# Fewer cached-key steps beside the attention, scans ahead of sums on VectorE, and norm rows in PSUM for the last output layer

## The chip, the core and the metric

The kernel runs on one core of one Trainium2 chip. The metric is device time of one launch in microseconds; a lower one is better. TensorE (PE) multiplies matrices into PSUM, VectorE (DVE) and ScalarE (ACT) read and write PSUM and SBUF, GpSimd (POOL) works in SBUF alone, and SyncE (SP) issues nearly all DMAs from one queue in order.

## The reference

One inference step of a two-layer trunk of width 1024, for a prompt of 1024 positions and for 8 samples with one new position each. Both groups share the weights. Layer 0 projects to q, k, v, a gate, a pooling input u and its gate. The attention is stick-breaking, with 8 heads of 64:

```
z = q.k / 8 + bias
w[t,s] = sigmoid(z[t,s]) * prod over s<j<t of (1 - sigmoid(z[t,j]))
o_a = w @ v ;  o_b = pooled(u) @ w_pool * scale
x1  = layer_norm(ALPHA*x + concat(o_a*silu(g_a), o_b*silu(g_b)) @ w_out)
```

For a sample, the keys and values are 4096 cached rows in 32 pages found through a page table. Layer 1 is a gated depthwise convolution of 31 taps with a layer norm and SiLU, a gate, an output projection and again `layer_norm(ALPHA*x + ...)`. Outputs are both groups' rows, the new k and v, and the pooling and convolution states.

## The kernel before

Matrix products in float32 are made of three products of split operands (`whi*xh + wlo*xh + whi*xl`, L225 to L227 and L1029 to L1031). ACT makes the high part, POOL (or DVE) the low part `wlo` (L210) or `xl` (L196).

Instructions of PE, ACT, DVE and POOL stand in the order in which the program writes them; each engine takes them in that order. So a waiting instruction holds up all that is behind it on its engine.

**The attention stage** (L947 to L981) goes through 48 units of up to 512 keys, 12 for each of four pairs of heads. For a unit, `z_a` has PE form scores and ACT form two sigmoids for each of two heads. `z_b` has DVE run the product scan (L365) and the product with the sigmoid (L369, L371) into `sg`. One unit later `tpart` transposes `sg` on PE (L845), and two units later `ppart` multiplies with v (L861). Between these slots, `fill.part` runs pieces of the projection of later heads.

**The decode of cached keys** is a generator, `decode_k`. `tick(n)` advances it by n steps. A full step issues the DMA of two pages of keys (`kt`, 512 KB, four buffers), multiplies the pages that were issued two steps earlier by the query row (L417), and sums products of the step before that over each head on DVE (L409). There are 64 full steps for each of two halves of the samples. The multiplication is on POOL in 7 of 8 steps and on DVE in the eighth (`KMOD`, `KPOOL`). A half ends with about ten short steps: transposes, sigmoids, one scan over 1024 elements (L437), carries between rows (L443 to L447), and one product over 1023 (L454).

In the stage a unit gets `TBASE + TSLOPE*(384-n)/384` steps for n keys. Over the 48 units this comes to 134 steps; 8 are made before the stage, and each half has 77, and one step stands ahead of them. The steps that are left then go one by one between the 32 groups of layer 0's output projection (`out_layer`, `between`), and the rest behind them.

**`out_layer`** does 32 groups, each of 24 matmuls for 128 rows by 256 columns. DVE adds the residual (L1062) and collects statistics (L1066). After a block's fourth group the norm follows: `norm_s` on DVE and POOL (`rs`, L1001, L1002), `norm_a` on DVE, `norm_b` on ACT and POOL (L1020, L1021), or on DVE (L1018) for the blocks in `FAST`. In layer 0 the gain row is in PSUM (`gps`); in layer 1 it is in SBUF. Weight quarters are converted by `conv_w` at groups 0 to 3 and 12 to 19.

**Between convolution and layer 1's output** the means and variances are spread over partitions by PE (`mid_a`), applied by DVE (`mid_b`), then SiLU, gate and split follow. `mid_a` takes its PSUM tile from `trp()`, which has two buffers there and four after `swap_psum("pzd", 4)`. The convolution's accumulator has its own two banks under the tag `conv`.

Of the kernel before, what the change touches and what calls it, by code (L numbers as in the profile page):

```python
# [14 lines left out]
F32 = mybir.dt.float32  # L15
# [3 lines left out]
AF = mybir.ActivationFunctionType  # L19
ALU = mybir.AluOpType  # L20
AX = mybir.AxisListType
SP = mybir.EngineType.SP
PSUM = bass.MemoryType.PSUM

P = 128
D = 1024
S = 1024
# [18 lines left out]
KS = 30  # L46
PS_ = 15
NEG = -1e30
KMOD = 8
KPOOL = 7  # L50
ENG = mybir.EngineType
KLAG = 2
DTB = 2
# [12 lines left out]
WRB = 3  # L66
ETICK = 0.35
EDVE = (1, 2, 3, 0)
TBASE = 2.8
TSLOPE = 1.5  # L70
NHEADS = (0, 6, 6, 6, 6, 6, 6, 6)
SNY = 7
# [12 lines left out]
SNZ = 5  # L85
HALVES = (3, 6)
OLAG = 3
FAST = (5, 6, 7)
WCONVA = ((0, 5), (1, 5))
SY = 2  # L90
VRATE = 1.575
# [9 lines left out]
def kernel(  # L101
# [9 lines left out]
    pe, act, dve, gp, sp = nc.tensor, nc.scalar, nc.vector, nc.gpsimd, nc.sync  # L111
# [8 lines left out]
    w_out1 = w_out_c[0]  # L120
# [11 lines left out]
    pz = [pap.enter_context(tc.tile_pool(name="pza", bufs=1, space=PSUM))]  # L132
    NZT = [5]

    def psum(tag, bufs, shape=(P, 512), dt=F32):
        return (psq[0] if tag == "qv" else ps).tile(list(shape), dt, tag=tag, name=tag, bufs=bufs)
# [3 lines left out]
    def acc():  # L140
        deep[1] += 1
        if deep[0] and deep[1] % deep[0] == 0:
            return trp()
        return psum("acc", 2)

    def trp():
        return pz[0].tile([P, 512], F32, tag="zt", name="zt", bufs=NZT[0])

    def swap_psum(name, n):
        pzp.close()  # L150
        pz[0] = pzp.enter_context(tc.tile_pool(name=name, bufs=1, space=PSUM, reuse_waits="tile"))
        NZT[0] = n
# [236 lines left out]
    def decode_k():  # L389
        qrow = {0: query_rows(0)}  # L390
        yield
        for hf in range(2):
# [5 lines left out]
            for s in range(len(units) + KLAG + 1):  # L398
# [13 lines left out]
                if KLAG <= s < len(units) + KLAG:  # L412
                    bi, j = units[s - KLAG]
                    b = hf * 4 + bi
                    kt = kts[s - KLAG]
                    eng = gp if (j // 2) % KMOD < KPOOL else dve
                    eng.tensor_tensor(out=kt, in0=kt, in1=qrow[b], op=ALU.mult)  # L417
# [53 lines left out]
    def tick(n):  # L471
        while n > 0 and queue:
            try:
                next(queue[0])
                n -= 1
            except StopIteration:
                queue.pop(0)
# [353 lines left out]
    def z_b(u):  # L831
        pair, qb, c0, c1, first, last = units[u]
        for hh in range(2):
            z, kp = st["z", u][hh]
            st["w", u, hh], st["prev", hh] = stick_b(z, kp, c1 - c0, None if first else st["prev", hh])
# [56 lines left out]
    t = trp()  # L892
# [23 lines left out]
    for i, q in enumerate(qorder):  # L916
# [3 lines left out]
        o = acc()[:, 0:n]  # L920
# [26 lines left out]
    for u in range(len(units) + 2):  # L947
        if u < len(units):
            pair, qb, c0, c1, first, last = units[u]
            n = c1 - c0  # L950
            if u % 12 == 0:
                fill.until(f"v{pair}")
                fleft = 42 if pair < 3 else 45
                fbase = fleft / 12.0
            fcred += fbase
            tcred += TBASE + TSLOPE * (384 - n) / 384.0
            z_a(u)
        k = int(tcred)
        tcred -= k
        f = min(int(fcred), fleft)  # L960
        fcred -= f
        fleft -= f
        fs = [(f + 2 - i) // 3 for i in range(3)]

        def slot(i):
            if i == PAT and u > 1:
                ppart(u - 2)
            if i == TAT and 0 < u <= len(units):
                tpart(u - 1)

        slot(0)
        fill.part(fs[0])
        tick((k + 1) // 2)
        if u < len(units):
            z_b(u)
        slot(1)
        fill.part(fs[1])
        slot(2)
        tick(k // 2)
        fill.part(fs[2])  # L980
        slot(3)  # L981
# [23 lines left out]
    def norm_a(gb, y, mv, halves, gps):  # L1005
        if gps:
            for i in range(2):
                h = slice(i * 512, i * 512 + 512)
                dve.scalar_tensor_tensor(out=y[:, h], in0=y[:, h], scalar=mv[:, 0:1], in1=gps[i],
                                         op0=ALU.subtract, op1=ALU.mult)  # L1010
            return
        for h in halves:
            dve.scalar_tensor_tensor(out=y[:, h], in0=y[:, h], scalar=mv[:, 0:1], in1=gb[:, 0, h],
                                     op0=ALU.subtract, op1=ALU.mult)

    def norm_b(gb, y, rs, fast, h):
        if fast:
            dve.scalar_tensor_tensor(out=y[:, h], in0=y[:, h], scalar=rs, in1=gb[:, 1, h], op0=ALU.mult, op1=ALU.add)  # L1018
        else:
            act.activation(out=y[:, h], in_=y[:, h], func=AF.Copy, scale=rs)  # L1020
            gp.tensor_tensor(out=y[:, h], in0=y[:, h], in1=gb[:, 1, h], op=ALU.add)  # L1021
# [10 lines left out]

    def out_layer(w, first, ahead, X, gb, pool, finish, between, before=None, half=None, tail=None, lag=OLAG, fast0=FAST, wide=0, gps=()):
        order = [(n4, tb) for t0 in (0, 4) for n4 in range(2) for tb in range(t0, t0 + 4)]
        for i in range(NTB + lag):
            if i < NTB:
                order.append((2, i))
            if i >= lag:
                order.append((3, i - lag))
        dmas = {0: (1, 3)} | {9 + i: (2, i) for i in range(4)} | {13 + i: (3, i) for i in range(4)}  # L1040
        convs = {i: (1, i) for i in range(4)} | {12 + i: (2, i) for i in range(4)} | {16 + i: (3, i) for i in range(4)}
        raws, sts = {}, {}
        tiles = {0: first, 1: [], 2: [], 3: []}

        def fetch(q, i):
            raws[q, i] = dma_quarter(w, q, i)

        for i in range(3):
            raws[1, i] = ahead[i]
        for s, (n4, tb) in enumerate(order):  # L1050
            f0 = n4 * 256
            if s in convs:
                q, i = convs[s]
                tiles[q].append(conv_w(raws[q, i], 2, 256, pool if q % 2 else None, dve if q == 1 and i % 2 and fast0 is FASTB else None))
            if s in dmas:
                fetch(*dmas[s])
            if before is not None:
                before(n4, tb)
            o = (trp() if s < wide and s % 3 else acc())[:, 0:256]
            out_group(tiles[n4], o, tb, half)  # L1060
            y = X[tb]
            dve.scalar_tensor_tensor(out=y[:, f0:f0 + 256], in0=y[:, f0:f0 + 256], scalar=ALPHA,  # L1062
                                     in1=o, op0=ALU.mult, op1=ALU.add)
            if n4 == 0:
                sts[tb] = pool.tile([P, 4, 6], F32, tag="st", name="st", bufs=NTB)
            dve.bn_stats(sts[tb][:, n4, :], y[:, f0:f0 + 256])  # L1066
            if n4 == 3:
                fast = tb in fast0
                halves = (slice(0, 512), slice(512, 1024)) if tb >= 6 else (slice(0, 1024),)
                mv, rs = norm_s(pool, sts[tb])  # L1070

                def app(y=y, mv=mv, rs=rs, tb=tb, fast=fast, halves=halves):
                    norm_a(gb[0], y, mv, halves, gps)
                    for h in halves:
                        norm_b(gb[0], y, rs, fast, h)
                        finish(tb, y, h)
                defer((DTC if fast0 is FASTB else DTD)[tb], app)
            between(n4, tb)
            point()
            if tail is not None:  # L1080
                tail(n4, tb)
# [4 lines left out]
    X = {}  # L1086
# [80 lines left out]
    rows = [(w_out0, 0, k) for k in range(NK)]  # L1167
# [347 lines left out]
    BC = {}  # L1515
# [34 lines left out]

    def mid_a(c):
        a, b = MID[c]
        t = trp()
        for i, tb in enumerate(range(a, b)):
            pe.transpose(out=t[:, i * P:(i + 1) * P], in_=rmf[:, tb:tb + 1].broadcast_to([P, P]), identity=ident)
            pe.transpose(out=t[:, 256 + i * P:256 + (i + 1) * P], in_=rvf[:, tb:tb + 1].broadcast_to([P, P]),
                         identity=ident)
        BC[c] = t
# [31 lines left out]
    X = {}  # L1590
# [5 lines left out]
            X[tb] = C[:, tb].rearrange("p k c -> p (k c)")  # L1596
            sp.dma_start(X[tb], x1_dram[tb * P:(tb + 1) * P, :])

    gb1 = [None]

    def before(n4, tb):
        if (n4, tb) in STEPS:
            STEPS[n4, tb]()
        if n4:
            return
        if tb == 3:
            gb1[0] = G[:, 0:2].rearrange("p t k c -> p t (k c)")
            sp.dma_start(gb1[0][:, 0, :], ln_c_g.to_broadcast([P, D]))
            sp.dma_start(gb1[0][:, 1, :], ln_c_b.to_broadcast([P, D]))
# [22 lines left out]
    mid_c(0)  # L1632
    mid_g(1)
    flush()
    swap_psum("pzd", 4)
    cxp.close()
    dx = ctx.enter_context(tc.tile_pool(name="dx", bufs=1, reuse_waits="tile"))
    fill.part(2)
# [9 lines left out]
    first1 = load_first(w_out1, range(2)) + late1  # L1648
    ahead1 = [dma_quarter(w_out1, 1, i) for i in range(3)]
# [3 lines left out]
    mid_g(2)  # L1653
    flush()
    deep[0] = DEEPD
    out_layer(w_out1, first1, ahead1, X, gb1, dx, fin1, lambda n4, tb: tick(1), before, lambda: tick(1))
    while queue:
        tick(1)
    flush()
# [24 lines left out]
```

## Time and profile before

| | us |
|---|---|
| median of 3 runs | 1143.98 |
| lowest and highest | 1140.2 and 1145.24 |
| the profiled execution | 1143.3 |
| its span, first to last instruction | 1141.5 |

| engine | busy us | share of span |
|---|---|---|
| PE | 1051.7 | 92% |
| DVE | 812.6 | 71% |
| POOL | 665.1 | 58% |
| ACT | 491.9 | 43% |

Times count from the span's start. The attention stage runs from about 68 to 497, layer 0's output projection from about 515 to 625, the convolution layer from there to about 1000, and layer 1's output projection to the end. Busy time is an average over these stages, so each is read by itself. PE's mean granted clock over the span is 0.971 of its upper level.

### The profile page before, as it was taken

To read this page: it belongs to the slowest core of one execution; us is meant where nothing else is said; L and a number is where in the kernel's file an instruction comes from. 1 tells how busy PE (TensorE), PEld (TensorE's weight loads), DVE (VectorE), ACT (ScalarE), POOL (GpSimd) and SP (SyncE) were. 2 spreads that over 40 slices of the span, in tenths; PEclk is the share of its full clock that TensorE was granted. 3 is DMA by queue.
4 is the path that set the end of the run, shared out by engine and by line. 5 is a ranking of instruction groups with operands and counts; after the bars stand their busy time and mean duration, and the time that the engine had idled before them with its cause. 6 is when DMAs were issued, how large, how long until landed. Compare 5 with 4: busy or idle time off the path is not lost.

```text
span 1141.5 us, 19830 instructions
## 1 busy us (share of the span) xinstructions
PE 1051.7 (92%) x6804; PEld 841.7 (74%) x6804; DVE 812.6 (71%) x961; ACT 491.9 (43%) x929; POOL 665.1 (58%) x502
## 2 busy tenths in 40 slices
PE   8998888889999998797998999999999999899994
PEld 7897777768877877697997666566666466677784
DVE  3458878688599898767348399999999960484246
ACT  4345465547565565571204224444544422462210
POOL 3277879691788889872418336765766612343235
PEclk9999999999999999898999999999999999899997
DMA  8577767783467976655203887787687678386922
GB/s 267 170 230 231 243 194 222 207 251 98 141 217 219 278 216 216 199 194 203 68 26 142 240 253 249 234 252 217 194 266 236 210 237 264 122 280 218 322 102 113
DMA packets 179206, 235.20 MB, mean 206 GB/s; under 512 B 15418, under 2 KB 95939, under 8 KB 179081
## 3 DMA queue, kind: packets, MB, share of 16 engines
q1 hardware_dynamic: 179105, 233.94, 65.1%
q8 instruction: 53, 0.87, 0.3%
q14 instruction: 48, 0.39, 0.1%
HBM read 212.60 MB, written 16.14 MB: 200 GB/s over the span
## 4 chain that ended last, share of the span: by engine, by line
PE 54%; POOL 13%; DVE 11%; issue 9%; DMA 7%; ACT 3%; SPq 3%; POOLq 0%; DVEq 0%; ACTq 0%
PE acc L225 11%; PE acc L227 10%; PE acc L226 10%; POOL kt L417 7%; PE qv L1151 5%; DMA kt<-in_cache_k_dram 3%; DVE zw L409 3%; PE acc L1029 3%; POOL wlo L210 2%; PE acc L1031 2%; PE acc L1030 2%; DVE kp L365 2%; DMA vt<-in_cache_v_dram 1%; DVE xl L196 1%; POOL xres L1021 1%
## 5 line engine op out<-in xcount | busy, mean ns | idle before, releaser
L225 PE MATMUL acc<-xh,whi 128*128 128x384 f32 (+2 forms) x960 | 361.5, 377 | 11.5 <-DVE hbt L705 5.7
L227 PE MATMUL acc<-xl,whi 128*128 128x384 f32 (+2 forms) x960 | 340.4, 355 | 0.2 <-DVE xl L196 0.2
L226 PE MATMUL acc<-xh,wlo 128*128 128x384 f32 (+2 forms) x960 | 339.7, 354 | 0.0
L417 POOL TENSOR_TENSOR kt<-kt,qbs 128x1024 f32<-128x1024 f32 x112 | 274.1, 2464 | 39.6 <-DMA kt<-in_cache_k_dram 30.0
L210 POOL TENSOR_TENSOR wlo<-wraw,whi 128x512 fp32r<-128x512 f32 x122 | 161.6, 1328 | 184.1 <-ACT whi L205 179.5
L1373 DVE SCALAR_TENSOR_TENSOR conv_acc<-hbuf,wdwT,conv_acc 128x1024 f32<-128x1024 f32 x196 | 252.8, 1290 | 6.8
L225 PEld LDWEIGHTS acc<-xh,whi 128*128 128x128 f32 x960 | 184.3, 192 | 78.1 <-issue 26.1
L409 DVE TENSOR_REDUCE zw<-kt 128x16 f32<-128x1024 f32 x128 | 153.6, 1212 | 63.5 <-POOL kt L417 63.3
L227 PEld LDWEIGHTS acc<-xl,whi 128*128 128x128 f32 x960 | 184.3, 192 | 18.0 <-DVE xl L196 0.7
L226 PEld LDWEIGHTS acc<-xh,wlo 128*128 128x128 f32 x960 | 185.0, 193 | 15.7 <-issue 0.3
L1363 POOL TENSOR_TENSOR conv<-conv,tap 128x512 f32<-128x512 f32 x84 | 105.9, 1293 | 17.6 <-ACT tap L1360 17.6
L1029 PE MATMUL acc<-whi,xh 128*128 128x256 f32 x352 | 102.4, 291 | 0.0
L1031 PE MATMUL acc<-whi,xl 128*128 128x256 f32 x352 | 99.5, 283 | 2.1 <-DVE xl L196 2.1
L1030 PE MATMUL acc<-wlo,xh 128*128 128x256 f32 x352 | 99.4, 282 | 0.0
L365 DVE TENSOR_TENSOR_SCAN kp<-kp,zt 128x512 f32<-128x512 f32 (+3 forms) x96 | 92.4, 963 | 1.2 <-ACT zt L361 1.2
L205 ACT ACTIVATE whi<-wraw 128x512 fp32r<-128x512 f32 x126 | 77.4, 624 | 32.1 <-DMA wraw<-in_w_out_ab_dram 14.1
L360 ACT ACTIVATE kp<-zt,nbiash 128x512 f32<-128x512 f32 (+3 forms) x96 | 55.8, 581 | 71.4 <-DVE sg L371 40.7
L1360 ACT ACTIVATE tap<-hbuf,wdwT 128x512 f32<-128x512 f32 x84 | 59.7, 721 | 48.0 <-POOL conv L1363 38.1
L1151 PE MATMUL qv<-vt,zw 128*32 128x512 f32 x512 | 76.1, 604 | 3.1 <-DMA vt<-in_cache_v_dram 3.1
L1029 PEld LDWEIGHTS acc<-whi,xh 128*128 128x128 f32 x352 | 66.8, 190 | 7.9 <-issue 7.4
L1031 PEld LDWEIGHTS acc<-whi,xl 128*128 128x128 f32 x352 | 67.0, 190 | 2.3 <-DVE xl L196 2.3
L845 PE MATMUL zt<-ident,sg 128*128 128x128 f32 x288 | 44.7, 286 | 24.2 <-DVE sg L371 12.9
(274 smaller groups left out, 1507.3 us busy)
## 6 DMA issues: line engine op xcount, KB each, us to landing
kt<-in_cache_k_dram SPq DMA_DIRECT2D x256, 256.0 KB
vt<-in_cache_v_dram SPq DMA_DIRECT2D x256, 256.0 KB
wraw<-in_w_in_c_dram SPq DMA_DIRECT2D x48, 256.0 KB
vt<-in_w_in_c_dram SPq DMA_DIRECT2D x48, 256.0 KB
wraw<-in_w_in_ab_dram SPq DMA_DIRECT2D x46, 256.0 KB
xt<-in_x_prompt_dram SPq DMA_DIRECT2D x8, 512.0 KB
wraw<-in_w_out_ab_dram SPq DMA_DIRECT2D x16, 256.0 KB
xres<-in_x_prompt_dram SPq DMA_DIRECT2D x8, 512.0 KB
```

The costliest lines, as they stand in the source:

```text
L210: (eng or gp).tensor_tensor(out=lo, in0=raw, in1=hi.bitcast(F32), op=ALU.subtract)
L225: pe.matmul(o, hi[:, k % 4, :], xh, start=(k == 0), stop=False)
L226: pe.matmul(o, lo[:, k % 4, :], xh, start=False, stop=False)
L227: pe.matmul(o, hi[:, k % 4, :], xl, start=False, stop=(k == NK - 1))
L365: dve.tensor_tensor_scan(out=kr, data0=kr, data1=z[:, 0:1].broadcast_to([P, n]), initial=1.0 if prev is None else prev, op0=ALU.mult, op1= ...
L409: dve.tensor_reduce(out=seg[:, j // 8, j % 8:j % 8 + 2, bi * 8:bi * 8 + 8], in_=kts.pop(s - KLAG - 1).rearrange("p a (h d) -> p a h d", d=DH),
L417: eng.tensor_tensor(out=kt, in0=kt, in1=qrow[b], op=ALU.mult)
L1029: pe.matmul(o, XH[:, k, cs], hi[:, k % 2, :], start=(k == 0), stop=False)
L1030: pe.matmul(o, XH[:, k, cs], lo[:, k % 2, :], start=False, stop=False)
L1031: pe.matmul(o, XL[:, k, cs], hi[:, k % 2, :], start=False, stop=(k == NK - 1))
L1151: pe.matmul(pv[32 * bi:32 * bi + 32, :], Z[:, j % 8 * 4 + j // 8, :], vts[bi], start=(j == 0), stop=(j == NPG - 1), tile_position=(0, 32 * ...
L1373: dve.scalar_tensor_tensor(out=part[1], in0=hb[:, j:j + S], scalar=w, in1=part[1], op0=ALU.mult, op1=ALU.add)
```

## The change

It changes four things. In the decode, every fourth multiplication goes to DVE (before, every eighth), and a unit gets a base of 2.35 steps (before 2.8): 112 steps in the stage for 134. Within a unit, `z_b` stands ahead of the first `tick`. In layer 1's output projection the gain row is copied to two PSUM banks and `norm_a` reads it there; blocks 5 and 7 use the new `norm_fast`, which keeps the value between its two passes in PSUM, and block 6 leaves the blocks whose second pass is on DVE. For these banks `trp()` has three buffers for four there, and `mid_a` of the first two parts writes to the convolution's two banks.

```diff
-KMOD = 8
-KPOOL = 7
+KMOD = 4
+KPOOL = 3
-TBASE = 2.8
+TBASE = 2.35
-FAST = (5, 6, 7)
+FAST = (5, 7)
...
         fill.part(fs[0])
-        tick((k + 1) // 2)
         if u < len(units):
             z_b(u)
+        tick((k + 1) // 2)
         slot(1)
...
+    def norm_fast(gb, y, mv, rs, h, i, gps):
+        t = trp()
+        dve.scalar_tensor_tensor(out=t, in0=y[:, h], scalar=mv[:, 0:1], in1=gps[i], op0=ALU.subtract, op1=ALU.mult)
+        return lambda: dve.scalar_tensor_tensor(out=y[:, h], in0=t, scalar=rs, in1=gb[:, 1, h], op0=ALU.mult, op1=ALU.add)
...
                 def app(y=y, mv=mv, rs=rs, tb=tb, fast=fast, halves=halves):
+                    if fast and gps:
+                        hs = (slice(0, 512), slice(512, 1024))
+                        bs = [norm_fast(gb[0], y, mv, rs, h, i, gps) for i, h in enumerate(hs)]
+                        for h, b in zip(hs, bs):
+                            b()
+                            finish(tb, y, h)
+                        return
                     norm_a(gb[0], y, mv, halves, gps)
...
     def mid_a(c):
         a, b = MID[c]
-        t = trp()
+        if c == 0:
+            BC["wide"] = pz[0].tile([P, S], F32, tag="conv", name="rows", bufs=1)
+        t = BC["wide"][:, c * 512:c * 512 + 512] if c < 2 else trp()
...
+        if (n4, tb) == (2, 4):
+            gps1.extend((psum("o", 1), pg.tile([P, 512], F32, name="scale1")))
+            for i in range(2):
+                act.activation(out=gps1[i], in_=gb1[0][:, 0, i * 512:i * 512 + 512], func=AF.Copy)
...
-    swap_psum("pzd", 4)
+    swap_psum("pzd", 3)
+    pg = ctx.enter_context(tc.tile_pool(name="pg", bufs=1, space=PSUM, reuse_waits="tile"))
...
-    out_layer(w_out1, first1, ahead1, X, gb1, dx, fin1, lambda n4, tb: tick(1), before, lambda: tick(1))
+    out_layer(w_out1, first1, ahead1, X, gb1, dx, fin1, lambda n4, tb: tick(1), before, lambda: tick(1), gps=gps1)
```

## Rows read from the trace of the kernel before

**Rows 1.** Three stretches: busy PE, PEld, DVE, ACT, POOL; PE clock; DMA share, GB/s.

```profile
68.00:497.00 429.00, 382.92 (x2621) 332.13 (x2620) 343.00 (x416) 240.93 (x504) 334.61 (x183) 0.96 0.69 213
531.00:590.00 59.00, 59.00 (x493) 58.83 (x493) 19.80 (x43) 9.57 (x18) 12.80 (x13) 0.99 0.21 67
590.00:640.00 50.00, 45.80 (x312) 39.81 (x310) 32.23 (x57) 20.39 (x32) 32.62 (x43) 1.00 0.46 153
```

**Rows 2.** Waits of PE, 68 to 497: us in total, times, longest.

```profile
PE zt L845 <- DVE sg L371: 12.9, 7, 3.2
PE zt L845 <- DVE sg L369: 10.8, 10, 2.4
PE acc L225 <- DVE hbt L705: 5.7, 4, 2.3
PE acc L225 <- DVE kl L611: 5.5, 2, 3.4
PE zt L815 <- DVE sg L371: 4.9, 1, 4.9
```

**Rows 3.** Waits of DVE, 68 to 497.

```profile
DVE zw L409 <- POOL kt L417: 60.2, 32, 5.4
...
DVE kp L365 <- ACT zt L361: 1.2, 1, 1.2
```

**Rows 4.** Timeline of DVE in one unit: start, us, instruction, idle before.

```profile
193.45 1.22 DVE L409 TENSOR_REDUCE zw<-kt 128x16 f32<-128x1024 f32 x1 [3.34 <-POOL kt L417]
```

**Rows 5.** Groups by line, 75 to 525: count, busy, mean ns, idle before.

```profile
L417 POOL TENSOR_TENSOR kt<-kt,qbs 128x1024 f32<-128x1024 f32 x106 | 259.9, 2469 | 39.3 <-DMA kt<-in_cache_k_dram 29.7 <-DVE kp L365 3.9 <-DVE zw L409 3.2
...
L409 DVE TENSOR_REDUCE zw<-kt 128x16 f32<-128x1024 f32 x123 | 147.7, 1212 | 57.4 <-POOL kt L417 57.1
...
L417 DVE TENSOR_TENSOR kt<-kt,qbs 128x1024 f32<-128x1024 f32 x16 | 28.1, 1756 | 0.0
```

**Rows 6.** The decode's multiplication, line 417: count, ns min/median/max.

```profile
L417 POOL TENSOR_TENSOR kt<-kt,qbs x112: 2337/2392/3387, 54.2 to 515.4; 128x1024 f32<-128x1024 f32 x112
L417 DVE TENSOR_TENSOR kt<-kt,qbs x16: 1209/1276/3224, 79.5 to 524.8; 128x1024 f32<-128x1024 f32 x16
```

**Rows 7.** Timeline of PE: first score product, four units apart.

```profile
274.50 0.63 PE L815 MATMUL zt<-km,qh 128*128 128x512 f32 x2
...
305.91 0.62 PE L815 MATMUL zt<-km,qh 128*128 128x512 f32 x2
```

**Rows 8.** Timeline of DVE in layer 0's output groups.

```profile
538.34 2.27 DVE L437 TENSOR_TENSOR_SCAN kpd<-kpd 128x1024 f32<-128x1024 f32 x1
...
546.15 0.42 DVE L1062 SCALAR_TENSOR_TENSOR xres<-xres,acc 128x256 f32<-128x256 f32 x1 [2.06 <-PE acc L1031]
546.61 0.43 DVE L1066 BATCH_NORM_STATS2 st<-xres 128x6 f32<-128x256 f32 x1
...
552.62 1.27 DVE L454 SCALAR_TENSOR_TENSOR zw<-kpd,car,zw 128x1023 f32<-128x1023 f32 x1
```

**Rows 9.** Timeline of POOL, layer 0's output groups.

```profile
559.98 1.29 POOL L210 TENSOR_TENSOR wlo<-wraw,whi 128x512 fp32r<-128x512 f32 x1 [3.70 <-ACT whi L205]
```

**Rows 10.** Timeline of SP's queue, start of layer 0's output groups.

```profile
508.08 11.08 SPq L1092 DMA_DIRECT2D xres<-in_x_prompt_dram  x2
```

**Rows 11.** Timeline of DVE: a norm's first pass from PSUM, then the end.

```profile
590.78 0.73 DVE L1009 SCALAR_TENSOR_TENSOR xres<-xres,mv,o 128x512 f32<-128x512 f32 x1
...
1118.98 1.27 DVE L1013 SCALAR_TENSOR_TENSOR conv<-conv,mv,gate 128x1024 f32<-128x1024 f32 x1
...
1122.67 3.58 DVE L1013 SCALAR_TENSOR_TENSOR conv<-conv,mv,gate 128x1024 f32<-128x1024 f32 x2
...
1137.09 1.41 DVE L1018 SCALAR_TENSOR_TENSOR conv<-conv,rs,gate 128x512 f32<-128x512 f32 x2 [0.45 <-POOL rs L1002]
```

**Rows 12.** Timeline of PE between convolution and layer 1's output.

```profile
987.79 0.45 PE L1555 MATMUL zt<-ident,rmu 128*128 128x128 f32 x1 [5.68 <-DVE conv L1567]
...
1012.30 0.38 PE L1031 MATMUL acc<-whi,xl 128*128 128x256 f32 x1 [2.09 <-DVE xl L196]
```

More of the change, by code (lines that the diff above doesn't have):

```diff
@@ L1597, in mid_c @@
             sp.dma_start(X[tb], x1_dram[tb * P:(tb + 1) * P, :])
-    gb1 = [None]
+    gb1, gps1 = [None], []
     def before(n4, tb):
```

## The prediction

> **What bounds the kernel now.** I read the stretches first. The attention stage lasts 429 us, and TensorE is busy for 383 of it [rows 1]; the other 46 us are what a change of order can win there. DVE is busy for 343 us and POOL for 335. Next come TensorE's waits in that stretch: 12.9 + 10.8 + 4.9 = 28.6 us for `sg`, the outcome of a unit's scans, and 5.7 + 5.5 = 11.2 us for two smaller results of DVE [rows 2]. So 39.8 of the 46 us are waits for DVE. Then DVE's own waits: it sits for 60.2 us in front of the decode's sum, waiting for POOL's multiplication, and for 1.2 us before a scan whose sigmoid is late [rows 3]. Busy and held together DVE is taken for about 403 of 429 us. The timeline shows how one becomes the other: at 193.45 a sum starts after 3.34 us of waiting for POOL, and the scans stand behind it in program order [rows 4]. The stage is bound by a chain of POOL, DVE and TensorE, each full at other moments, and not by TensorE's work.
>
> What it could reach: between the halves of the decode, where few sums are made, four units take 305.91 - 274.50 = 31.4 us, or 7.85 us each [rows 7], against 429 / 48 = 8.94 on average. Over 48 units that is 52 us less.
>
> Behind the stage, layer 0's output groups are bound by TensorE: 59.00 of 59 us, with POOL busy for 12.8 and the DMA moving 67 GB/s [rows 1].
>
> All sums stand against the profiled execution: 1143.3 us, its span of 1141.5 and 1.8 around it. The median of the runs is 0.7 above it, so no correction is made.
>
> **The change part by part.**
>
> *Decode in the stage.* 134 - 112 = 22 steps leave it. Each takes a sum of 1.212 us off DVE [rows 5]: 26.7 us. Of the multiplications, 106 were on POOL and 16 on DVE [rows 5], 122 in all; 100 stay, 75 on POOL and 25 on DVE. POOL goes from 259.9 to 75 x 2.469 = 185 us, which is 75 less. DVE gets 9 more of them at 1.756 us, the mean of the sixteen [rows 5] (the median is 1.276, the longest 3.224 [rows 6]): 15.8 us. DVE's net is 26.7 - 15.8 = 11 us less. POOL falls from 78% of the stage to about 61%, so it is seldom behind when a sum asks for it.
>
> The multiplications on DVE run between 1.209 and 3.224 us; the longest exceeds the shortest by 2.0 us, a little less than one multiplication of POOL (2.392) [rows 6]. The Trainium skill (SBUF — State Buffer, Who interferes with whom) says that a DVE instruction with both inputs in SBUF shares a read port with GpSimd, and that whichever comes second waits for the whole of the other. The spread of the rows agrees with it. By that rule each of the 9 could cost 3.224 in place of 1.756, 13 us more on DVE.
>
> *Scans first.* The scans then no longer stand behind a sum that waits for POOL. The 28.6 us of waits for `sg` should nearly go; the 11.2 us for the two other results stay, since these still stand behind sums. I take 25 us for both edits together. Bounds: 52 us if every unit runs at 7.85 us; 0 if DVE now idles in front of the scans, since the sums that covered the sigmoids (1.2 us of waits now [rows 3]) stand behind. What is late next is the small results of DVE, then TensorE itself.
>
> *The decode in layer 0's output.* 120 steps are done before it (8 + 112), where it was 142. One step stands ahead and the first half takes 77, so the second half stands at 42 of its 64 fetches: 24 multiplications and 25 sums remain, where 2 and 3 remained. They go one to a group, through group 24 of 32, and the half's short steps fall on groups 25 to 31 and into the next layer's start. TensorE makes 493 matmuls in 59 us [rows 1], at 24 to a group that is 2.87 us for one. DVE needs 0.42 + 0.43 + 1.21 + 1.28 / 4 = 2.4 us of that, POOL 0.75 x 2.39, and 1.28 / 4 more as a bound if it stands still while DVE multiplies, 2.1 [rows 5, 6, 8]. Both fit, the base cost is nothing, and TensorE covers it. Three places don't fit:
> - The start: SP's queue stands for 11.08 us on a residual load [rows 10], and the keys' loads stand behind it. The first multiplications here come late, DVE waits with its sum, and behind it wait residual additions that free PSUM. I take 2 us (0 to 8).
> - Groups 12 to 19, where POOL also makes eight `wlo` of 1.29 us [rows 9]: 8 x (2.1 + 1.29) = 27.1 against 8 x 2.87 = 23.0, 4.1 us behind. One group's lag (2.87) is allowed between a multiplication and its sum, so 2 us (0 to 5).
> - The end: the scan (2.27) and the product (1.27) [rows 8], 3.5 us on DVE, now fall where the norms run, a stretch in which TensorE is busy for 45.8 of 50 us and DVE and POOL for 32 each [rows 1]. Transposes on TensorE and small carries on POOL wait for them in order. I take 4 us (0 to 9).
>
> Sum: 8 us lost (0 to 22).
>
> *Norm rows and the end.* From 1122.67 DVE does two first passes in 3.58 us, where one alone takes 1.27, and its last operation ends at 1138.5 [rows 11]. With the gain in PSUM a pass is 2 x 0.73 = 1.46 us [rows 11]. After: blocks 4 and 5, 1.46 + 1.46 + 2 x 0.74 = 4.4 to 1127.1; block 6, addition, statistics and their sum at some 0.4 each [rows 8], 1.2, and 1.46, to 1129.7; block 7 the same, to 1132.4; its `rs` comes behind block 6's two additions on POOL, 2 x 1.29 by the nearest row of that size [rows 9], so not before 1132.3, and later by ACT's pass ahead of them and by `rs` itself: I take 1133.8; then 1.5 to 1135.3. That is 3 us less (bounds: 5 less without the wait for `rs`; 2 more if POOL's additions take twice as long and end last).
>
> *The rows in the convolution's banks, and three buffers for four.* TensorE stands 5.68 us in front of `mid_a` at 987.79, and later 2.09 us for the split of a later block at 1012.30 [rows 12]. DVE's line of work between is not shortened, so time won at the first place is lost at the second: nothing (2 less to 2 more).
>
> Sum: 1143.3 - 25 + 8 - 3 = 1123.3, so 1123.
>
> **The rivals.**
> - *TensorE becomes the bound in the stage.* All units take 7.85 us: 1143.3 - 52 + 8 - 3 = 1096; with the 11.2 us that stay, 1107, which I take. For it: the stretch that ran so. Against: it had few sums. Chance 0.14.
> - *Scans first only moves the wait.* DVE idles before the scans, and the gain is the smaller number of steps alone: 22 of 134 of the 60.2 us, 10 us. 1143.3 - 10 + 8 - 3 = 1138. For it: DVE's total hardly falls. Against: the scans wait for sigmoids for 1.2 us in all now [rows 3]. Chance 0.18.
> - *The shared port takes it back.* All 25 multiplications cost 3.224 us: 25 x (3.224 - 1.756) = 37 us more on DVE than summed above; with a third of that on the path, as an estimate, 12 us are lost: 1135. For it: the longest row. Against: the median of 1.276 [rows 6]. Chance 0.09. The rule of the Trainium skill named above (SBUF — State Buffer, Who interferes with whom) is this rival's, taken at its extreme.
> - *Slower: the loads of keys hold layer 0's output.* In the stage POOL waited 29.7 us for keys over 106 multiplications [rows 5]. If SP's queue, full of weights and residuals, lets each of 25 steps come 1.4 us late, DVE's additions come late with them and a group takes 4.3 us: 35 us and the 4 of the end, so 1143.3 - 25 - 3 + 39 = 1154. It decides from about 1 us a step on, (25 + 3 - 4) / 25. Against: 67 GB/s there [rows 1]. Chance 0.13.
>
> **How the numbers follow.** The forecast holds 0.46. Less than 0.5% (5.7 us) can't be told from no change: the bounds are 1138.3 and 1149.7. Faster: 0.45 + 0.14 + half of 0.18 + 0.08 = 0.76. Same: the other half, 0.09, with 0.04 from edges of the others, 0.13. Slower 0.11. The range leaves out most of the slow rival and a part of the fast one: 1105 to 1141. The forecast's own range is 1112 to 1134.
>
> **What would show it.** Right: in the stage DVE's wait for POOL below 25 us, TensorE's wait for `sg` below 6, and a stage of about 404 us; output groups of layer 0 near 2.87 us each but for groups 0 to 4 and 12 to 19; first passes of 0.73 us, with DVE's last operation about 11 us behind TensorE's last. Wrong: a scan that waits for its sigmoid for tens of us (second rival); DVE multiplications near 3 us (third); residual additions that wait for a sum, and TensorE for these, along layer 0's groups (fourth).

## The result and the profile after

The changed kernel takes 1108.53 us (median; 1105.11 to 1113.35) against 1144.59 before: a ratio of 0.970, with an interval of 0.965 to 0.974. The profiled execution took 1110.31 us, its span is 1108.5, 33.0 less than before. In a second series it was at 1111.84 (ratio 0.973, 0.970 to 0.976). The forecast was 1123, so the sign and the range (1105 to 1141) were right and the size was too small: 36 us for 20. The forecast's own narrower range, 1112 to 1134, was missed.

The places where the 33.0 us of the span come from, by the first and last instructions of a line in each trace:

| stretch | before | after | change |
|---|---|---|---|
| start to the stage's last product with v | 495.6 | 452.0 | -43.6 |
| from there to layer 0's first residual addition | 24.8 | 25.9 | +1.1 |
| to its last residual addition (32 groups) | 96.8 | 103.5 | +6.7 |
| to the last transposes for layer 1 | 14.8 | 22.0 | +7.2 |
| to the end | 509.5 | 505.1 | -4.4 |

The stretches of the changed kernel, with the columns of [rows 1], are the attention stage, most of layer 0's groups, and the change of layer:

```profile
68.00:453.00 385.00, 368.80 (x2622) 325.73 (x2621) 329.74 (x405) 240.06 (x503) 260.90 (x150) 0.99 0.69 211
...
490.00:545.00 55.00, 54.65 (x460) 54.44 (x459) 44.56 (x65) 6.07 (x10) 46.15 (x22) 1.00 0.81 267
545.00:600.00 55.00, 43.88 (x286) 40.53 (x285) 37.65 (x60) 22.01 (x34) 35.16 (x49) 0.88 0.34 119
```

The stage answers to the first row of [rows 1]. POOL's busy time falls by 74 us and DVE's by 13, as the sum said (75 and 11). TensorE is idle for 16 us where it was for 46. And its busy time for the same matmuls fell from 382.9 to 368.8, since the granted clock rose from 0.96 to 0.99: 14 us that the sum did not contain. Read in steps of 2 us, the clock falls to about 0.5 of full (1.2 GHz) eight times in the stage of the kernel before, each time behind idle time of TensorE, and twice in the changed kernel. One such place before, with the columns of [rows 1]:

```profile
204.00:206.00 2.00, 0.00 (x0) 0.00 (x0) 1.97 (x3) 0.61 (x2) 2.00 (x3) 1.00 0.36 123
...
210.00:212.00 2.00, 2.00 (x12) 2.00 (x11) 2.00 (x2) 0.66 (x2) 0.00 (x0) 0.53 0.89 294
```

The second row of the changed kernel shows POOL at 46 of 55 us, where it was busy for 12.8 of 59 [rows 1], with TensorE still full.

TensorE's waits in the stage, against [rows 2]:

```profile
PE zt L815 <- issue: 4.0, 2, 2.1
PE zt L713 <- DVE hbt L705: 3.8, 1, 3.8
PE zt L815 <- DVE sg L371: 2.2, 2, 1.6
...
PE acc L225 <- DVE hbt L705: 1.4, 2, 1.0
...
PE zt L845 <- DVE sg L369: 0.2, 1, 0.2
```

The waits for `sg` went from 28.6 us to 2.4, and the wait for `kl` is gone. DVE's own waits in the stage, against [rows 3]:

```profile
DVE zw L409 <- POOL kt L417: 16.3, 16, 2.8
...
DVE kp L365 <- ACT zt L361: 6.1, 6, 2.5
```

The wait for POOL fell from 60.2 us to 16.3, and the price of putting the scans first is seen in the second line: 6.1 us in front of a late sigmoid, for 1.2.

TensorE's timeline behind the stage, with the idle time at the end of a line and what ended it; these lines are from the start of layer 0's groups and from the change of layer:

```profile
482.03 0.58 PE L1035 MATMUL zt<-wlo,xh 128*128 128x256 f32 x1 [6.02 <-DVE wlo L210]
486.44 0.58 PE L1035 MATMUL zt<-wlo,xh 128*128 128x256 f32 x1 [1.49 <-DVE wlo L210]
...
575.34 1.72 PE L1138 MATMUL zt<-ident,xres 128*128 128x128 f32 x8 [4.12 <-POOL xres L1026]
585.24 0.19 PE L451 MATMUL zt<-ident,crow 1*128 1x1 f32 x1 [2.12 <-DVE xl L196]
592.06 1.70 PE L463 MATMUL zt<-ident,zw 128*128 128x128 f32 x8 [2.56 <-DVE xl L196]
```

The last two are steps of the decode's end that now stand among the norms; the profile puts the end of both waits down to a split (`xl`) on DVE. DVE's timeline at the change of layer has the scan and the product of [rows 8]:

```profile
564.88 4.25 DVE L437 TENSOR_TENSOR_SCAN kpd<-kpd 128x1024 f32<-128x1024 f32 x1
...
589.10 2.19 DVE L454 SCALAR_TENSOR_TENSOR zw<-kpd,car,zw 128x1023 f32<-128x1023 f32 x1
```

They take 4.25 and 2.19 us beside POOL's work, where the scan took 2.27 with POOL idle and the product 1.27. The wait of 4.12 us above hangs on this scan: DVE makes the block's first pass behind it, at 570.23, then come ACT's pass and POOL's addition, which ends where the transposes start.

Where the 6.7 us of the 32 groups were lost, DVE's residual additions show. These are the additions of group 26 (counted from 0) and of the last group, first before the change, then after it:

```profile
595.65 0.42 DVE L1062 SCALAR_TENSOR_TENSOR xres<-xres,acc 128x256 f32<-128x256 f32 x1 [1.65 <-PE acc L1031]
...
617.22 0.41 DVE L1062 SCALAR_TENSOR_TENSOR xres<-xres,acc 128x256 f32<-128x256 f32 x1
```

```profile
552.20 0.42 DVE L1067 SCALAR_TENSOR_TENSOR xres<-xres,acc 128x256 f32<-128x256 f32 x1 [0.36 <-PE acc L1036]
...
581.45 0.41 DVE L1067 SCALAR_TENSOR_TENSOR xres<-xres,acc 128x256 f32<-128x256 f32 x1
```

From the first addition to that of group 26 it is 75.3 us before and 74.3 after, so the groups beside the decode's multiplications and sums lose nothing. The last five groups take 21.6 us before and 29.3 after. With the change of layer that is 36.4 and 51.2: all that is lost in layer 0's output, 14.8 us, is lost where the decode's closing steps meet the norms.

The end of the changed kernel on DVE, against [rows 11]:

```profile
1093.15 0.68 DVE L1009 SCALAR_TENSOR_TENSOR conv<-conv,mv,o 128x512 f32<-128x512 f32 x1
1093.75 0.74 DVE L1009 SCALAR_TENSOR_TENSOR conv<-conv,mv,scale 128x512 f32<-128x512 f32 x1
1094.41 0.75 DVE L1018 SCALAR_TENSOR_TENSOR zt<-conv,mv,o 128x512 f32<-128x512 f32 x1
...
1104.20 1.41 DVE L1019 SCALAR_TENSOR_TENSOR conv<-zt,rs,gate 128x512 f32<-128x512 f32 x2 [1.32 <-POOL rs L1002]
```

Passes of 512 take 0.68 to 0.75 us, and the last wait is for `rs` (1.32 us), which stands behind block 6's additions on POOL, as the prediction had it.

Between convolution and layer 1's output, TensorE's two waits of [rows 12] are still there:

```profile
957.58 0.45 PE L1569 MATMUL zt<-ident,rmu 128*128 128x128 f32 x1 [5.24 <-DVE conv L1581]
...
982.12 0.58 PE L1036 MATMUL acc<-whi,xl 128*128 128x256 f32 x1 [2.22 <-DVE xl L196]
```

### The profile page after: what moved, and what is told of

The parts are those of the page before. It is cut to its first block, busy times and chain, and to the rows that moved or that the text cites. A ratio compares the mean times of both kernels' runs of the same rounds, so it can differ in the third digit from the quotient of the medians.

```text
span 1108.5 us, 19858 instructions
## 1 busy us (share of the span) xinstructions
PE 1042.0 (94%) x6804; PEld 840.1 (76%) x6804; DVE 833.3 (75%) x982; ACT 493.4 (45%) x933; POOL 632.2 (57%) x488
## 4 chain that ended last, share of the span: by engine, by line
PE 51%; POOL 7%; DVE 6%; DMA 5%; issue 2%; ACT 2%; SPq 2%; POOLq 0%; DVEq 0%; ACTq 0%
PE acc L225 10%; PE acc L227 9%; PE acc L226 9%; PE qv L1163 6%; DMA kt<-in_cache_k_dram 3%; POOL kt L417 2%; PE acc L1034 2%; PE acc L1036 2%; PE acc L1035 2%; DVE conv L1581 2%; PE zt L1034 1%; POOL wlo L210 1%; DVE xl L196 1%; PE qv L1199 1%; PE zt L1035 1%
## 5 line engine op out<-in xcount | busy, mean ns | idle before, releaser
L417 POOL TENSOR_TENSOR kt<-kt,qbs 128x1024 f32<-128x1024 f32 x96 | 237.8, 2487 | 79.0 <-DMA kt<-in_cache_k_dram 58.8
L1035 PEld LDWEIGHTS acc<-wlo,xh 128*128 128x128 f32 x352 | 68.5, 195 | 1.1 <-POOL wlo L210 1.0
```

Source lines behind the costliest of these rows:

```text
L1035: pe.matmul(o, XH[:, k, cs], lo[:, k % 2, :], start=False, stop=False)
```

## The experiments

The theory going in (A): scans stood behind sums that waited for POOL, the order and the lighter load both take away that one wait. The first rival (B): the load of the decode on POOL and DVE is what counts. The results by the same stretches as above (end of the stage, 32 groups, change of layer, rest), with the ratio to the kernel before:

| kernel | ratio (95%) | stage ends | groups | change | rest |
|---|---|---|---|---|---|
| before | 1 | 495.6 | 96.8 | 14.8 | 509.5 |
| order only | 0.987 (0.983 to 0.991) | 480.4 | 96.9 | 14.7 | 510.2 |
| split only | 1.007 (1.005 to 1.010) | 504.7 | 96.9 | 14.8 | 507.5 |
| rate only | 0.981 (0.977 to 0.984) | 455.1 | 107.8 | 24.6 | 511.2 |
| rate and split | 0.981 (0.977 to 0.986) | 457.0 | 103.4 | 23.9 | 510.4 |
| norm edits only | 1.001 (0.998 to 1.003) | 492.0 | 99.1 | 18.2 | 506.6 |
| changed, again | 0.973 (0.970 to 0.976) | 453.4 | 106.8 | 21.9 | 503.3 |
| changed, without the split | 0.973 (0.971 to 0.976) | 449.8 | 104.3 | 21.9 | 504.2 |
| changed, old second pass in layer 0 | 0.976 (0.973 to 0.978) | 452.9 | 103.3 | 23.8 | 504.9 |
| changed, early steps | 0.978 (0.976 to 0.980) | 466.5 | 101.1 | 14.7 | 506.2 |
| changed, early steps, base 2.2 | 0.990 (0.987 to 0.993) | 472.1 | 104.0 | 21.9 | 506.1 |
| changed, closing steps later | 0.972 (0.970 to 0.975) | 450.7 | 100.8 | 26.3 | 504.8 |

The stretches are read in one profiled execution of each kernel, and leave out the 20 to 26 us between the stage's end and the first residual addition. The executions of "norm edits only", "changed, without the split", "changed, early steps" and "changed, closing steps later" were the shortest of their runs, by 1 to 6 us under the median. The stage of "norm edits only" is the old one and ends 3.6 us earlier than before, so a difference of this size in that column shows nothing.

**Order only.** The kernel before, with

```diff
-        tick((k + 1) // 2)
         if u < len(units):
             z_b(u)
+        tick((k + 1) // 2)
```

> The kernel before, with one edit: a unit's scans are put ahead of the first decode steps. Theory A (scans were held up behind sums that waited for POOL): TensorE's waits for sg fall from 28.6 us to below 8, the attention stage from 429 us by 20 to 28, the run to about 1120. Theory B (the load of the decode on POOL and DVE is what counts, the order only moves the wait): DVE's waits before scans rise from 1.2 us to over 15, the stage falls by less than 6, the run stays above 1138.

It came to 1128.72 us. The stage's row and, below, TensorE's longest waits in it:

```profile
68.00:481.40 413.40, 379.87 (x2620) 331.76 (x2619) 344.11 (x416) 240.09 (x503) 332.21 (x183) 0.97 0.71 218
```

```profile
PE acc L225 <- DVE kl L611: 6.2, 2, 3.5
PE acc L225 <- DVE hbt L705: 5.7, 4, 2.6
PE zt L845 <- DVE sg L371: 4.1, 5, 1.3
```

The waits for `sg` fell to 7.6 us in all, but the waits that still stand behind sums stayed, and the stage gave 15 us, less than theory A asked for. DVE's wait for POOL fell as well, from 60.2 us to 43.6, by about what the stage gave. DVE's wait before scans rose to 2.6 us only, so B's form of the order, that it merely moves the wait, is wrong as well.

**Rate and split, without the order.** `TBASE` 2.35, `KMOD` 4, `KPOOL` 3.

> The kernel before, with fewer decode steps to a unit (base 2.35 for 2.8) and every fourth multiplication on DVE, the order as before. Theory A: about half of the waits for sg go (28.6 to 12 or 15), the stage falls by 15 to 22, layer 0's output projection and the change to layer 1 cost about 15 more, so the run is at 1135 to 1143. Theory B: the stage falls by 35 or more without the new order, and the run is at 1120 or less.

The run is at 1121.74 us and the stage is 39 us shorter: this is what B expected of the stage, and A's share was far too small. The run misses B's 1120 by 2 us, as the groups and the change of layer cost 16 us. Which of the two edits does it was left open by this run; the next two tell.

**Split only.**

```diff
-KMOD = 8
-KPOOL = 7
+KMOD = 4
+KPOOL = 3
```

> The kernel before with one edit: every fourth multiplication on DVE. Theory A (POOL's lateness is what counts, and one multiplication of 2.4 us on POOL is worth more than one of 1.2 to 1.8 on DVE): DVE's wait for POOL falls from 60 to below 40 us, the stage by 10 to 18 us, the run is at 1125 to 1133. Theory B (only the smaller number of steps counts): the stage changes by less than 5 us.

Slower, 1150.44 us, which neither theory had. The stage and DVE's wait for POOL:

```profile
68.00:505.70 437.70, 386.51 (x2620) 334.07 (x2619) 371.57 (x432) 240.48 (x503) 304.74 (x167) 0.96 0.68 207
```

```profile
DVE zw L409 <- POOL kt L417: 38.4, 20, 5.4
```

The wait fell by 22 us as A said, but DVE's own work rose by 28.6 [rows 1]: busy and held together are 410 us for 403, and the stage is 9 us longer. TensorE's waits for `sg` rose from 28.6 us to 32.3. It is read so: a sum that waits less is worth nothing if the multiplications that DVE takes over stand ahead of the scans in its place. How much of the harm is the number of these and how much their length was not tried: DVE's 31 multiplications in the stage take 57.0 us, a mean of 1.839, where the shortest takes 1.210.

**Rate only.**

```diff
-TBASE = 2.8
+TBASE = 2.35
```

> The kernel before with one edit: a base of 2.35 decode steps to a unit for 2.8. The theory as it now stands (the stage lasts as long as DVE is busy or held by POOL, until TensorE's work is reached near 360 us; steps taken away free both engines, a multiplication moved to DVE only passes the load on): the stage falls by 25 to 40 us with the old split, layer 0's output and the change of layer cost about 14, the run is at 1115 to 1130. Rival (fewer steps need the new split as well): the stage falls by less than 20.

As expected: 1124.09 us, and the stage alone is 40.5 us shorter, just above the 25 to 40 expected.

```profile
68.00:456.10 388.10, 367.48 (x2616) 321.06 (x2616) 311.67 (x392) 239.19 (x502) 284.36 (x163) 1.00 0.68 208
```

DVE is busy for 312 us and held for 42.6, together 354. TensorE's busy time falls by 15 us with the clock at 1.00, and its waits from 45.6 to 20.2. The rate is most of the gain, and it pays for it behind the stage with 21 us (groups 11, change of layer 10), where 14 were expected.

**No decode in the stage.** `TBASE` and `TSLOPE` 0: every step is made behind the stage, so only the stage is of interest.

> The changed kernel with no decode step in the attention stage: all are made behind it, so its total time is of no interest and the stage's length is. Theory A (in the changed kernel the decode is nearly out of TensorE's way): the stage takes 370 to 382 us, little less than the 385 of the changed kernel, at a granted clock of 0.99 or more. Theory B (its load still costs much): 365 us or less.

```profile
68.00:428.10 360.10, 358.46 (x2598) 319.47 (x2598) 169.64 (x278) 236.62 (x494) 74.32 (x72) 1.00 0.27 76
```

This kernel was run once, and took 1324.84 us in all. The stage takes 360 us, TensorE has hardly a gap left, and even the low guess of B was met. So the decode still costs some 25 us in the changed kernel's stage, and the bound that the prediction drew from four units (7.85 us each, 377 us) was too high by 17.

**Changed, without the split.** `KMOD` 8 and `KPOOL` 7 in the changed kernel.

> The changed kernel with every eighth multiplication on DVE again. Theory A (DVE's load counts more than POOL's): DVE's busy time in the stage falls by about 15 us, its waits for POOL rise by 10 to 15 us, the stage stays within 5 us of 385 and the run within 6 of the changed kernel. Rival (with fewer steps POOL's lateness decides): the stage is 10 us or more longer, and layer 0's groups, where POOL would need 2.2 to 3.5 us of 2.87, are longer by 5 or more.

1112.18 us against 1111.84 and 1108.53 for the changed kernel: the same. DVE's busy time fell by 18.7 us (329.7 to 311.0) and its wait for POOL rose by 15.6 (16.3 to 31.9), about the trade that theory A described. The groups of layer 0 are no longer either. With fewer steps the split is neither gain nor loss.

**Norm edits only.** The changed kernel with the old order, rate and split.

> The kernel before, with the norm's edits alone (gain row in PSUM, the new second pass, block 6 on ACT and POOL, rows in the convolution's banks, three PSUM buffers for four). Theory A: the end is shorter by 2 to 4 us and nothing else moves: 1140 to 1142. Rival: the third buffer's loss or POOL's additions at the end take it back: 1144 to 1147.

No difference in time (1143.78 us against 1142.64). The trace shows a gain and a loss: from layer 1's mean transposes to the end it is 169.9 us for 173.5 before, 3.6 less, and the change of layer is 18.2 for 14.8, 3.4 more. TensorE's timeline there shows the loss:

```profile
619.99 1.31 PE L1138 MATMUL zt<-ident,xres 128*128 128x128 f32 x8 [4.25 <-DVE xres L1019]
```

Layer 0's `out_layer` also has its gain row in PSUM, so the new second pass applies to its block 7, and it takes two of the four buffers that block 6's transposes need next. They wait for block 7's second pass.

**Changed, old second pass in layer 0.**

```diff
-                    if fast and gps:
+                    if fast and gps and fast0 is not FASTB:
```

> The changed kernel, with the new second pass kept out of layer 0's output (there it also fell on block 7). Theory A (block 7's two PSUM tiles hold up the transposes of block 6, which cost 3.4 us in the run with the norm's edits alone): TensorE's wait for that second pass goes and the change of layer is 2 to 4 us shorter, the run 2 to 4 us faster than the changed kernel. Rival (here the decode's product and transposes are late anyway): no difference above 1 us.

The rival held: 1112.61 against 1111.84 us, and the change of layer is 23.8 for 21.9. In the changed kernel other steps are late there anyway: the last five groups and the change together are 51.6 us, for 51.2.

**Changed, early steps** (with the old second pass in layer 0). `ETICK` 0.65 for 0.35.

> As the run without the new pass in layer 0, and with 0.65 decode steps for 0.35 to a piece of the first projections, ahead of the attention stage (15 for 8). Theory A (the decode's end collides with the norms at the change of layer, and TensorE, POOL and DVE have room ahead of the stage): the short steps fall on groups 18 to 24, the change of layer falls from 22 to 15 or 16 us, and the run is 5 to 8 us faster than the changed kernel. Rival: the keys' loads delay the first weights and the first projections take 5 us or more longer, and nothing is won.

Half right. With the closing steps ahead of the norms the change of layer fell from 23.8 us to 14.7, what it was before the change, and the last five groups from 27.7 to 22.3. Together they are 37.0 us, for 36.4 before the change and 51 to 52 in the changed kernel and its variants without early steps. That shows where those 15 us were lost. But the rival's delay came as well: the first product with v starts at 99.1 us for 84.7, and from there to the last it is 367 us, as in the changed kernel. The largest of TensorE's waits in the stage is for a copy of the query's parts:

```profile
PE zt L815 <- DMA qh<-qh: 7.0, 2, 6.0
```

The run's 1115.97 us are 3.4 above the same kernel without early steps (1112.61), with intervals that overlap: nothing is won.

**Changed, early steps and a base of 2.2.**

> The changed kernel with 0.65 decode steps for 0.35 to a piece of the first projections (7 more there) and a base of 2.2 for 2.35 (7 fewer in the stage), so that the same number is left behind the stage. If a step costs 1.5 to 1.8 us of the stage, it falls by 10 to 13; the first projections cost 4 to 6 more, as in the run with early steps; the change of layer stays at 22. The run is then 4 to 8 us faster than the changed kernel, at 1101 to 1107. Rival: the stage does not fall by more than the start loses, as it nears TensorE's own work, and the run is within 3 us of the changed kernel.

Wrong by far: 1130.83 us. The third unit was held up, as in the run before, and TensorE's timeline shows it:

```profile
98.21 1.01 PE L815 MATMUL zt<-km,qh 128*128 128x384 f32 x2 [6.61 <-DMA qh<-qh]
```

The copy of the query's parts waits in the one queue of DMAs, among the keys' loads: just ahead of it the queue stands for 6.94 us on four of these. The first product with v starts at 100.1 us, 15 us late. The closing steps still stand among the norms, and the last five groups and the change are 51.5 us, as in the changed kernel. Besides, from the first product with v to the last (100.1 to 472.1) it is 372 us for 367 in the changed kernel, with 7 steps fewer; why the stage did not fall there stays unexplained.

**Changed, closing steps later.**

```diff
-            for _ in range(SY):
+            for _ in range(SY + 6 * hf):
```

> The changed kernel, with six empty steps ahead of the second half's closing steps, so that its transposes, sigmoids, scan and product come behind layer 0's 32 groups, among the first pieces of layer 1, and no longer among the norms. Theory A (the closing steps lengthen the change of layer by their collision with the norms on ACT, DVE and POOL): the scan takes 2.3 us in place of 4.25, from the last residual addition to the last transposes it is 15 to 18 us in place of 22, the run 3 to 7 us faster than the changed kernel, at 1103 to 1108. Rival (the closing chain of TensorE, ACT and DVE is as long wherever it stands, and TensorE waits for it in order): the change is shorter, but layer 1's first pieces lose as much, and the run is within 2 us of the changed kernel.

The rival held in the time: 1110.17 us, within 2 of the changed kernel. The scan is back at 2.28 us, with POOL idle beside it,

```profile
L437 DVE TENSOR_TENSOR_SCAN kpd<-kpd x2: 2280/2280/2280, 279.3 to 590.0; 128x1024 f32<-128x1024 f32 x2
```

and the groups are at 100.8, but the change is 26.3, longer and not shorter as both theories had it. The last five groups and the change are 51.0 us together, as in the changed kernel, so the scan's collision is not what the end costs. TensorE stands in order before links of the closing chain: 2.5 us for the scan, and 3.9 before its first transposes, until block 7's second pass frees their PSUM. The chain cost the same here as among the norms; only early steps, which put it where TensorE had other groups to do, took that cost away. No version here beat the changed kernel by more than the intervals.

## Why the prediction was right, and by which steps

*The stage* was the term that was mis-sized: 25 us forecast, 43.6 measured, inside its bounds of 0 to 52. The step that failed is the sentence that "the other 46 us are what a change of order can win there". TensorE's idle time fell by 30 us, and its busy time by 14, since behind a wait the same work runs for a while at the lower clock and counts as more busy time. Less waiting gives both back. The 11.2 us of waits for two small results that the sum kept fell too: that for `kl` is gone, and those for `hbt` come to 5.2.

*What does it* was put wrongly too. The sum credited the two edits together and leaned on the order, while alone the order gives 15 us of the stage and the rate 40; together 43.6, as the rate alone leaves TensorE only 20 us of waits. The split was credited with POOL's relief; alone it makes the kernel slower by 0.7%, and in the changed kernel it does nothing.

*The shared port* cost less than the sum allowed: the 26 multiplications on DVE in the stage have a mean of 1.482 us, below the 1.756 of before. Against the shortest, 1.212, that is 7 us of DVE's time in all.

*Layer 0's output* cost 15 us for a forecast of 8, inside its bounds of 0 to 22, but in one of its three places only. The start was to cost 2 us and groups 12 to 19 another 2. TensorE's two waits for `wlo` at the start are 7.5 us for 6.1 before, yet groups 0 to 26 together take 1.0 us less than before (2.7 more in the second series), and TensorE is busy for 54.65 of 55 us through groups 12 to 19. The end was to cost 4 us, at most 9, and cost 14.8. Its mechanism was named rightly, TensorE and POOL waiting in order, but it was priced by 3.5 us of DVE's work, and what counted was the length of the whole closing chain, with TensorE idle for 11 of 55 us and its clock at 0.88; early steps, which move the chain, remove the loss.

*The end* was right in its own stretch: from layer 1's mean transposes to the end 170.7 us for 173.5, 2.8 less for a forecast of 3; DVE ends 7.9 us behind TensorE's last matmul (before 11.3). The "about 11 us" among the signs to look for was a slip; the sum's own 1135.3 meant 8. The step that was missed is the new pass in layer 0, which takes back 3.4 us when the norm's edits stand alone; in the changed kernel leaving it out shows no gain.

*The middle*: nothing was forecast, and from the mean transposes to layer 1's first addition it is 45.4 us in both.

*The rivals*: that TensorE becomes the bound came nearest, at 1107 with TensorE busy for 369 of 385 us. The slower one did not come: groups 0 to 26 took 2.86 us each (74.3 / 26) and not 4.3, and the longer ones behind them come from the closing steps and not from the keys' loads.

*Luck.* The stage gave 19 us more than forecast and layer 0's output cost 7 more. The two errors have opposite signs, so the total came nearer than its parts.

## What to carry to other kernels

Where several engines take turns at holding a stage, add busy time and time held of each: the stage followed DVE's sum of work and waits for POOL (before 403 us, split only 410, order only 388, rate only 354, changed 346, for stages of 429, 438, 413, 388 and 385) until TensorE's own work was near. Idle time of TensorE understates what a smoother stage gives, when its clock sinks with the waits. An edit that moves work from a late engine to a nearly full one must be tried alone: here it was the one part of a good change that did harm by itself. Price a chain of short steps that several engines take in turn by its whole length, and not by one engine's work in it.

## What the runs showed of the hardware

A scan over 1024 elements in SBUF took 4.25 us when it started during an addition on POOL, and 2.28 without one; POOL's `rs` beside it took 2.21 us where it takes 0.22, as POOL's timeline of the changed kernel shows:

```profile
564.59 2.39 POOL L1026 TENSOR_TENSOR xres<-xres,lngb 128x1024 f32<-128x1024 f32 x1 [1.53 <-ACT xres L1025]
566.94 2.21 POOL L1001 TENSOR_SCALAR rs<-mv 128x1 f32<-128x1 f32 x1
```

The scan starts at 564.88 and ends at 569.13, 2.15 us after POOL's addition (566.98), and POOL's next instruction ends with it. In the run with the old second pass in layer 0 the scan starts first, by 0.21 us, and then POOL pays:

```profile
567.40 2.23 DVE L437 TENSOR_TENSOR_SCAN kpd<-kpd 128x1024 f32<-128x1024 f32 x1
```

```profile
567.61 4.18 POOL L1026 TENSOR_TENSOR xres<-xres,lngb 128x1024 f32<-128x1024 f32 x1 [1.53 <-ACT xres L1025]
```

The Trainium skill (SBUF — State Buffer, Who interferes with whom) states that a DVE instruction with two SBUF inputs contends with a GpSimd instruction that reads SBUF, and that issue order decides which of the two blocks. The scan, whose two inputs are one tile in SBUF, agrees with it in both orders.

After a wait of 6.02 us TensorE worked at its lower level: 0.50 of full, that is 1.2 GHz, between 483 and 490 in the changed kernel:

```profile
483.00:490.00 7.00, 5.51 (x26) 5.22 (x25) 6.93 (x9) 0.00 (x0) 2.37 (x1) 0.50 0.89 303
```
